# A decoder layer with 32 experts on one core: where in an expert pair the previous pair's combination is issued

## The chip, the cores and the metric

The kernel runs on one core of a Trainium2 chip. The metric is device microseconds of one execution. Engines are called by the profile's names: PE (TensorE matmul), PEld (its weight loads), DVE (VectorE), ACT (ScalarE), POOL (GpSimd) and SP (SyncE, which issues nearly all transfers here).

## The reference, cut to what matters

The layer is an attention mixer on 512 tokens of width 2048, and behind it a mixture of 32 experts. Only the experts matter here:

```
def hierarchical_moe(h, router_g, router_e, w_gate, w_up, w_down):
    ...   # each token: 1 group of 4, 2 of the group's 8 experts, weights `gate`
    def expert_block(args):
        xe, e = args
        u = jax.nn.silu(xe @ w_gate[e]) * (xe @ w_up[e])
        return u @ w_down[e]
    ...
    return jnp.zeros_like(h).at[buf_tok].add(yb * buf_w[:, None].astype(h.dtype))
x = x + g2 * y.reshape(B, S, D)
```

Every expert has three float32 matrices of 4 MB (2048x512, 2048x512, 512x2048). 512 tokens with two experts each make 1024 assignments.

## The kernel before, in words

The instructions of each engine, and the issues on its queue, stand in the order in which the program writes them (`tc.manual_schedule()`); the framework only adds the semaphore waits. Up to about 950 us the kernel does the modulation, the mixer and the router. Then 16 pairs of experts follow (`for n in range(NP)`). In a pair the first 64 columns of a tile belong to expert 2n and the other 64 to expert 2n+1, so that one pair takes up to 64 tokens of each of its experts. Tokens beyond that are done in the block behind `tc.If(reg > 0)`; `reg` counts such blocks, and it is zero for these inputs (no instruction of the block is in the trace).

The steps of pair n, in the order of the program:

- **gates and find.** `gates` (lines 1199 and 1201) computes the token weights of pair n on DVE; `find` (lines 1183 to 1192) builds for pair n+1 the one-hot matrix `oT` and the token indices on DVE, and POOL issues the gather of its rows into `xg` (line 1189).
- **g, in four steps c = 0 to 3.** Each takes two weight tiles of 1 MB (one of each expert) and eight matmuls, which the trace shows as 16 PE instructions of 512 columns. ACT then applies Silu (`gate_fn`).
- **u**, in four steps of the same size. Then `hidden` (DVE, line 1268), `hidden_t` (four PE transposes, line 1274, and an ACT copy to `uT`).
- **y**, in four steps f. In f = 0 and 1 there are also the transposes of the next pair's rows (`turn_x`, line 1211, `ga`), after `normed` (DVE, line 1205). The four sums `py` stand in the four PSUM banks of the tag "mm".
- **gated** (lines 1223 to 1225), once for each quarter q of the columns: DVE computes `yt` out of `py[q]`, ACT copies it to `yH`, DVE computes the rest `yL`.

The **combination** adds `yH + yL` to the tokens' rows: `add_pair` yields four times, once for each q; each time it issues eight PE matmuls (two for each token tile, `cb`) into the four banks of the same tag "mm", and four DVE additions into `acc` (line 1233). It is a generator, `done`, that the next pair advances. Before the change it advances after g step 2, after u step 1, after `hidden`, and after `hidden_t`:

```
                if (k, c) in (("g", 2), ("u", 1)):
                    next(done, None)
...
        u = hidden(sg, pgu[1])
        next(done, None)
        uT = hidden_t(u)
        next(done, None)
        flat(done)
```

The last pair works otherwise: its `w_down` is loaded by column parts, f is a column part, and `last_pair` combines and stores quarter by quarter (line 1247).

**SBUF slots.** All weight tiles and large buffers share 23 slots of 8 KB per partition (pool "big"). While y of a pair runs, ten are taken by the accumulators `acc` (4), the gate row, `rows`, `more`, the two `xg` and the next `xe`, and twelve by weight tiles loaded ahead: `need` loads up to 12 tiles beyond the one in use (`AH = 12`). `yH` takes the 23rd slot, when the last `w_down` tile leaves it. `yL` gets the slot that is given back next. `load_to` (line 256) issues the weight loads on SP, and each issue may wait for its slot and for an earlier transfer on its semaphore lane.

The counts of overflow blocks (`nbk`, `toti`) are computed behind all pairs, and `nc.values_load` (line 1359) reads the number into a register of every engine just before the `If`.

Of the kernel before, what the change touches and what calls it, by code (L numbers as in the profile page):

```python
# [14 lines left out]
I32 = mybir.dt.int32  # L15
AF = mybir.ActivationFunctionType
OP = mybir.AluOpType
AX = mybir.AxisListType
PSUM = bass.MemoryType.PSUM

P = 128
# [4 lines left out]
NE = 32  # L26
# [3 lines left out]
CAP = 64  # L30
# [47 lines left out]
def tile_hybrid_layer(ctx: ExitStack, tc, A, out, dbg=None):  # L78
    nc = tc.nc
    x, xT, w_mod, w_in, w_q_up, rel_bias, w_out = (  # L80
        A[k] for k in ("x", "xT", "w_mod", "w_in", "w_q_up", "rel_bias", "w_out"))
    w_gate, w_up, w_down = A["w_gate"], A["w_up"], A["w_down"]

    sm = ctx.enter_context(tc.tile_pool(name="sm", bufs=1))
# [4 lines left out]
    def slot(shape, dt=F32, name="b"):  # L89
        t = big.tile(shape, dt, name=name, tag="b")  # L90
        return t

    def bank(tag, name, dt=F32):
        t = ps.tile([P, 512], dt, name=name, tag=tag)
        return t

    V, G, T, SC, Q = nc.vector, nc.gpsimd, nc.tensor, nc.scalar, nc.sync

    def act(o, i, f=AF.Copy, **kw):
        return SC.activation(o, i, f, **kw)  # L100

    def mm(o, l, r, start, stop, skip=False):
        return T.matmul(o, l, r, start=start, stop=stop, skip_group_check=skip)  # L103
# [62 lines left out]
    w_g_v = w_gate.rearrange("e (c p j) f -> e c p j f", c=4, j=4)  # L166
    w_u_v = w_up.rearrange("e (c p j) f -> e c p j f", c=4, j=4)
    w_d_v = w_down.rearrange("e (j p) d -> e j p d", p=P)
    w_dc_v = w_down.rearrange("e (j p) d -> e p j d", p=P)

    SH1, SC1, G1, SH2, SC2, G2 = range(6)
    CUTS = {SC2: CUT[0], SH2: CUT[1], G1: CUT[2], G2: CUT[3]}
# [2 lines left out]
    def src(it):  # L175
        k = it[0]
        if k == "m":
            _, v, c, q = it
            if c is None:
                return w_mod_v[:, q, v * D:v * D + D], [P, D]  # L180
            o, n, r = PIECES[c]
            return w_mod_v[:, r * q:r * q + r, v * D + o:v * D + o + n], [P, r, n]
        if k == "A":
            _, c, h = it
            return w_in_v[c][:, h, :, 0:NA], [P, 2, NA]
        if k == "B":
            _, n, c = it
            return w_in_v[c][..., BCOL + 512 * n:BCOL + 512 * (n + 1)], [P, 2, 2, 512]
        if k == "Q":
            return w_q_v[:, :, 512 * it[1]:512 * (it[1] + 1)], [P, 4, 512]  # L190
        if k == "O":
            _, c, q = it
            return w_o_v[:, 4 * q:4 * q + 4, 512 * c:512 * (c + 1)], [P, 4, 512]
        if k == "g":
            return w_g_v[it[1], it[2]], [P, 4, 512]
        if k == "u":
            return w_u_v[it[1], it[2]], [P, 4, 512]
        if it[1] >= NE - 2:
            return w_dc_v[it[1]][..., 512 * it[2]:512 * it[2] + 512], [P, 4, 512]
        return w_d_v[it[1], it[2]], [P, D]  # L200


# [8 lines left out]
    for d, (o, n, r) in enumerate(PIECES):  # L211
# [3 lines left out]
        k = len(mod) // 2 if d else 0  # L215
# [853 lines left out]
    def st(shape, name):  # L1069
        return sm.tile(shape, F32, name=name)  # L1070
# [3 lines left out]
                    op=OP.mult)  # L1074
# [66 lines left out]
    cnt = st([P, 32], "cnt")  # L1141
# [62 lines left out]
    def normed(xs, g, cs=slice(0, D)):  # L1204
        V.tensor_scalar(xs[:, cs], xs[:, cs], g[:, 2:3], None, op0=OP.mult)  # L1205
# [47 lines left out]
    def need(i, k, e, c):  # L1253
        load_to(base + i + 1 + AH)
        return raw.pop((k, e, c))

    def flat(g):
        for _ in g:
            pass

    def gate_fn(pb):
        sg = sm.tile([P, S], F32, name="sg", tag="rb", bufs=2)
        act(sg, pb, AF.Silu)
        return sg

    def hidden(sg, pb):
        u = sm.tile([P, S], F32, name="u", tag="rb", bufs=2)
        V.tensor_tensor(u, sg, pb, op=OP.mult)  # L1268
        return u
# [9 lines left out]
    def down(py, uT, f, ws):  # L1279
        for r in range(2):  # L1280
            hs = slice(64 * r, 64 * r + 64)
            mm(py[hs], uT[:, 128 * f + 64 * r:128 * f + 64 * r + 64], ws[r], f == 0, f == 3, True)

    xe = slot([P, 16, P], name="xe")
    oT, g = find(slotk[:, 0:1], xg[0])
    make_row(rows[:, 2], gt[:, 0])
# [4 lines left out]
    done = iter(())  # L1291
    NP = NE // 2
    for n in range(NP):
        pgu = []
        i = 24 * n
        last = n == NP - 1
        for k in "gu":
            po = bank("at", k)
            pgu.append(po)
            if k == "g":  # L1300
                gate = gates(slotk[:, n:n + 1], g)
                if not last:
                    after = find(slotk[:, n + 1:n + 2], xg[(n + 1) % 2])
            for c in range(4):
                ws = [need(i + r, k, 2 * n + r, c) for r in range(2)]
                i += 2
                for j in range(4):
                    for r in range(2):
                        hs = slice(64 * r, 64 * r + 64)
                        mm(po[hs], xe[:, 4 * c + j, hs], ws[r][:, j], c == 0 and j == 0, c == 3 and j == 3, True)  # L1310
                if (k, c) in (("g", 2), ("u", 1)):
                    next(done, None)
            if k == "g":
                sg = gate_fn(po)
        u = hidden(sg, pgu[1])
        next(done, None)
        uT = hidden_t(u)
        next(done, None)
        flat(done)
        if not last:  # L1320
            normed(xg[(n + 1) % 2], after[1])
            xe = slot([P, 16, P], name="xe")
        py = [bank("mm", f"y{q}") for q in range(4)]
        if last:
            yH, yL = slot([P, D], F32R, name="yH"), slot([P, D], F32R, name="yL")
            done = last_pair(oT, yH, yL)
        for f in range(4):
            ws = [need(i + r, "d", 2 * n + r, f) for r in range(2)]
            i += 2
            if last:  # L1330
                for k in range(4):
                    down(py[f], uT, k, [w[:, k] for w in ws])
                gated(py[f], gate, yH, yL, f)
                for _ in range(4 if f else 0):
                    next(done)
                continue
            for q in range(4):
                down(py[q], uT, f, [w[:, 512 * q:512 * q + 512] for w in ws])
                if q % 2 and f < 2:
                    turn_x(xe, xg[(n + 1) % 2], 2 * f + q // 2)  # L1340
        if last:
            break
        yH, yL = slot([P, D], F32R, name="yH"), slot([P, D], F32R, name="yL")
        for q in range(4):
            gated(py[q], gate, yH, yL, q)
        done = add_pair(oT, yH, yL)
        oT, g = after
    flat(done)


    nbk = st([P, 32], "nbk")
    V.tensor_scalar(nbk, cnt, float(CAP), None, op0=OP.is_gt)
    for b in range(1, 4):
        V.scalar_tensor_tensor(nbk, cnt, float(CAP + 128 * b), nbk, op0=OP.is_gt, op1=OP.add)
    tot = st([P, 1], "tot")
    toti = sm.tile([P, 1], I32, name="toti")
    V.tensor_reduce(tot, nbk, axis=AX.X, op=OP.add)
    V.tensor_copy(toti, tot)
    reg = nc.values_load(toti[0:1, 0:1], min_val=0, max_val=16,
                         skip_runtime_bounds_check_because="1024 assignments fill under 16 such blocks")  # L1360
    with tc.If(reg > 0):
        ov = k2([P, 512], "ov")
        end = ov[:, 0:64].rearrange("p (i e) -> p i e", i=2)
# [4 lines left out]
        for i in range(5):  # L1368
            k, a, b = 1 << i, end[:, i % 2], end[:, (i + 1) % 2]
# [5 lines left out]
        with tc.For_i(0, reg, 1):  # L1375
# [15 lines left out]
                                skip_runtime_bounds_check_because="a count of experts that end before a block")  # L1391
            oT, g = find(oc[:, 4:5], xg[0])
            g = (g, gates(oc[:, 4:5], g))
# [52 lines left out]
def _prepare(inputs):  # L1446
    f = lambda n: np.asarray(inputs[n])
    fold = lambda v: v.reshape(4, 128, 4, -1).transpose(1, 0, 2, 3).reshape(128, -1)
    fold8 = lambda v: v.reshape(8, 128, 2).transpose(1, 0, 2).reshape(128, -1)
    tall = lambda v: v.reshape(-1, 128).T  # L1450
    bm = f("b_mod").reshape(6, 2048)
    vecs = np.concatenate(
        [fold8(bm[1]), fold8(bm[0]), fold(bm[4]), fold(bm[3]), fold8(f("ln1_g")), fold(f("ln2_g")),
         f("c").reshape(128, 16), tall(f("q_norm_g")), tall(f("q_gain")), tall(f("k_gain")), tall(f("gn_a")),
         tall(f("gn_b"))], axis=1)
    cst, ohd, flip = _constants()
    a = {
        "x": f("x").reshape(512, 2048), "xT": f("x").reshape(512, 2048).T, "w_mod": f("w_mod")[0],
        "w_in": f("w_in")[0], "w_q_up": f("w_q_up")[0], "rel_bias": f("rel_bias"),
        "w_out": f("w_out")[0], "w_gate": f("w_gate")[0], "w_up": f("w_up")[0], "w_down": f("w_down")[0],  # L1460
        "router": fold(np.concatenate([f("router_g")[0], f("router_e")[0]], axis=1)), "vecs": vecs, "b_gate": bm[[2, 5]], "cst": cst, "ohd": ohd, "flip": flip,
        "toki": np.tile(np.arange(512, dtype=np.float32) - AWAY, (128, 1)),
    }
    return {k: np.ascontiguousarray(v) for k, v in a.items()}
# [15 lines left out]
```

## Time and profile before

| | |
|---|---|
| Time, median of 3 runs | 1921.93 us (1921.22 to 1929.43) |
| The profiled execution | 1928.09 us, span 1926.2 us |
| Busy, share of the span | PE 92%, DVE 50%, ACT 31%, POOL 20% |
| Granted TensorE clock, mean | 0.978 |
| HBM traffic over the span | 583.60 MB read, 8.40 MB written |
| Weight loads of the experts | 384 transfers of 1024 KB on SP's queue |

The profile's page gives shares over the whole span, and the stages differ: the experts have the transfers at about 420 GB/s in slice after slice, the mixer does not. So the tables by window and the timelines of one pair say more than the shares. A busy PE is not a PE at its peak: each row's duration includes the drain of its pipeline, and the start of the next row is the better measure.

### The profile page before, as it was taken

To read this page: it belongs to the slowest core of one execution; us is meant where nothing else is said; L and a number is where in the kernel's file an instruction comes from. 1 tells how busy PE (TensorE), PEld (TensorE's weight loads), DVE (VectorE), ACT (ScalarE), POOL (GpSimd) and SP (SyncE) were. 2 spreads that over 40 slices of the span, in tenths; PEclk is the share of its full clock that TensorE was granted. 3 is DMA by queue.
4 is the path that set the end of the run, shared out by engine and by line. 5 is a ranking of instruction groups with operands and counts; after the bars stand their busy time and mean duration, and the time that the engine had idled before them with its cause. 6 is when DMAs were issued, how large, how long until landed. Compare 5 with 4: busy or idle time off the path is not lost.

```text
span 1926.2 us, 21350 instructions
## 1 busy us (share of the span) xinstructions
PE 1763.9 (92%) x8098; PEld 986.5 (51%) x8098; DVE 971.9 (50%) x1473; ACT 604.2 (31%) x1138; POOL 394.0 (20%) x307
## 2 busy tenths in 40 slices
PE   4999999999899998898799999999999999999997
PEld 1777777665677676786333333333333333333333
DVE  6888722378855668768322333423333343323325
ACT  3645444554547543443221101111021101211020
POOL 3543311333337326756000000000000000000000
PEclk8999999999999998999799999999999999999999
DMA  9878412323225647769499999999999999999997
GB/s 349 273 260 297 133 66 88 131 88 101 81 104 200 243 175 262 262 250 374 180 420 420 419 419 419 419 420 419 419 419 420 419 419 420 419 420 418 420 414 273
DMA packets 136427, 585.06 MB, mean 304 GB/s; under 512 B 10761, under 2 KB 43697, under 8 KB 78977
## 3 DMA queue, kind: packets, MB, share of 16 engines
q1 hardware_dynamic: 132240, 569.09, 75.3%
q0 software_dynamic: 4080, 14.57, 2.1%
q8 instruction: 65, 1.06, 0.2%
q14 instruction: 42, 0.34, 0.0%
HBM read 583.60 MB, written 8.40 MB: 307 GB/s over the span
## 4 chain that ended last, share of the span: by engine, by line
DMA 44%; PE 6%; DVE 1%; issue 0%; ACT 0%; SPq 0%; DVEq 0%
DMA w_u<-in_w_up 17%; DMA w_g<-in_w_gate 14%; DMA w_d<-in_w_down 14%; PE y L103 2%; PE u L103 2%; PE g L103 1%; PE cb L103 1%; PE ga L1211 0%; DVE x L1233 0%; DMA xg<-x1d,gi 0%; DVE xg L1205 0%; DVE u L1268 0%; PE uT L1274 0%; DVE yt L1223 0%; DVE yL L1225 0%
## 5 line engine op out<-in xcount | busy, mean ns | idle before, releaser
L103 PE MATMUL u<-w_u,xe 128*64 128x512 f32 x1024 | 270.0, 602 | 26.3 <-DMA w_u<-in_w_up 25.2
L103 PE MATMUL g<-w_g,xe 128*64 128x512 f32 x1024 | 242.2, 598 | 21.2 <-DMA w_g<-in_w_gate 21.2
L1233 DVE TENSOR_TENSOR x<-cb,x 128x512 f32<-128x512 f32 x256 | 157.3, 683 | 193.5 <-PE cb L103 193.4
L103 PE MATMUL y<-w_d,uT 128*64 128x512 f32 x1024 | 236.9, 600 | 0.7 <-ACT uT L100 0.7
L282 POOL TENSOR_TENSOR accv<-accv,w_m_None 128x768 f32<-128x768 f32 (+2 forms) x62 | 153.7, 2479 | 217.6 <-ACT w_m_None L100 138.6
L1189 POOL DMA_INDIRECT xg<-x1d,gi x16 | 16.1, 1006 | 875.6 <-DVE t L1192 634.2
L103 PEld LDWEIGHTS u<-w_u,xe 128*64 128x64 f32 x1024 | 79.5, 137 | 206.5 <-issue 135.8
L103 PEld LDWEIGHTS g<-w_g,xe 128*64 128x64 f32 x1024 | 77.1, 137 | 175.5 <-issue 129.3
L1223 DVE SCALAR_TENSOR_TENSOR yt<-y,gs,accv 128x512 f32<-128x512 f32 x64 | 47.8, 747 | 202.4 <-PE y L103 202.4
L280 DVE SCALAR_TENSOR_TENSOR accv<-w_m_None,sil,accv 128x1280 f32<-128x1280 f32 (+2 forms) x62 | 133.9, 2160 | 6.1 <-issue 5.4
L100 ACT ACTIVATE xe<-ga,modc 128x128 f32<-128x128 f32 x256 | 94.6, 465 | 119.8 <-PE y L103 92.6
L103 PEld LDWEIGHTS y<-w_d,uT 128*64 128x64 f32 x1024 | 66.6, 136 | 116.0 <-issue 107.9
L100 ACT ACTIVATE uT<-uT 128x512 f32<-128x512 f32 x16 | 9.6, 598 | 352.3 <-PE uT L1274 352.3
L103 PE MATMUL cb<-yH,oT 128*128 128x512 f32 x256 | 107.8, 421 | 0.9 <-DVE x L1233 0.9
L100 ACT ACTIVATE yH<-yt 128x512 fp32r<-128x512 f32 x64 | 40.4, 631 | 204.6 <-DVE yt L1223 121.5
L103 PE MATMUL cb<-yL,oT 128*128 128x512 f32 x256 | 101.0, 394 | 0.0
L1225 DVE TENSOR_TENSOR yL<-yt,yH 128x512 fp32r<-128x512 f32 x64 | 44.3, 692 | 110.5 <-PE g L103 52.8
L394 DVE TENSOR_TENSOR hl<-w_O,hl 128x1024 fp32r<-128x1024 f32 x32 | 67.8, 2122 | 40.6 <-ACT hl L100 31.7
L1268 DVE TENSOR_TENSOR u<-sg,u 128x512 f32<-128x512 f32 x16 | 11.0, 689 | 130.6 <-PE u L103 130.6
L282 POOL TENSOR_TENSOR acc<-acc,w_m 128x160 f32<-128x160 f32 x105 | 61.3, 584 | 71.5 <-ACT w_m L100 63.8
L103 PEld LDWEIGHTS cb<-yH,oT 128*128 128x128 f32 x256 | 48.2, 188 | 49.6 <-issue 39.5
L1211 PEld LDWEIGHTS ga<-cst,xg 128*128 128x128 f32 x256 | 36.8, 210 | 64.6 <-issue 43.9
(413 smaller groups left out, 3190.0 us busy)
## 6 DMA issues: line engine op xcount, KB each, us to landing
w_g<-in_w_gate SPq DMA_DIRECT2D x128, 1024.0 KB, 19.9
w_u<-in_w_up SPq DMA_DIRECT2D x128, 1024.0 KB, 21.2
w_d<-in_w_down SPq DMA_DIRECT2D x128, 1024.0 KB, 19.9
w_m_None<-in_w_mod SPq DMA_DIRECT2D x64, 1024.0 KB, 5.0
w_m<-in_w_mod SPq DMA_DIRECT2D x32, 1024.0 KB, 9.0
w_B<-in_w_in SPq DMA_DIRECT2D x48, 512.0 KB, 4.7
w_O<-in_w_out SPq DMA_DIRECT2D x16, 1024.0 KB, 5.5
w_A<-in_w_in SPq DMA_DIRECT2D x8, 848.0 KB, 11.3
```

The source lines that it names most:

```text
L100: return SC.activation(o, i, f, **kw)
L103: return T.matmul(o, l, r, start=start, stop=stop, skip_group_check=skip)
L280: V.scalar_tensor_tensor(acc[:, lo], w[:, lo], s, acc[:, lo], op0=OP.mult, op1=OP.add)
L282: G.tensor_tensor(acc[:, hi], acc[:, hi], w[:, hi], op=OP.add)
L394: low_eng[0].tensor_tensor(t[:, 1], s, t[:, 0].bitcast(F32), op=OP.subtract)
L1189: G.indirect_dma_start(xs, None, x1d[:, :], bass.IndirectOffsetOnAxis(ap=gi[:, 0:1], axis=0), bounds_check=S - 1, oob_is_err=False)
L1211: T.transpose(pb[:, 128 * j:128 * j + 128], xs[:, 512 * c:512 * c + 512].rearrange("p (k j) -> p j k", j=4)[:, j], ident)
L1223: V.scalar_tensor_tensor(yt, y, g, rowv[G2][:, cs], op0=OP.mult, op1=OP.mult)
L1225: V.tensor_tensor(yL[:, cs], yt, yH[:, cs].bitcast(F32), op=OP.subtract)
L1233: return lambda: V.tensor_tensor(acc[q][:, t], pb, acc[q][:, t], op=OP.add)
L1268: V.tensor_tensor(u, sg, pb, op=OP.mult)
```

## The change

Four edits:

- The combination of pair n-1 is advanced once after each of the four g steps of pair n, its matmuls and its additions alike; nothing of it is left for u, `hidden` or `hidden_t`.
- The counts of overflow blocks are computed at the head of pair 1.
- The registers are loaded at the head of the last pair, on all engines.
- The last pair's `w_down` comes from a new input `w_last`, which holds the two matrices by column parts; a partition then reads one run of 8 KB for a tile, where it read four runs of 2 KB.

```diff
         if it[1] >= NE - 2:
-            return w_dc_v[it[1]][..., 512 * it[2]:512 * it[2] + 512], [P, 4, 512]
+            return A["w_last"][it[1] - NE + 2, it[2]], [P, 4, 512]
...
+    nbk = st([P, 32], "nbk")
+    def blocks():
+        V.tensor_scalar(nbk, cnt, float(CAP), None, op0=OP.is_gt)
+        for b in range(1, 4):
+            V.scalar_tensor_tensor(nbk, cnt, float(CAP + 128 * b), nbk, op0=OP.is_gt, op1=OP.add)
+        tot = st([P, 1], "tot")
+        toti = sm.tile([P, 1], I32, name="toti")
+        V.tensor_reduce(tot, nbk, axis=AX.X, op=OP.add)
+        V.tensor_copy(toti, tot)
+        return toti
...
     for n in range(NP):
+        if n == 1:
+            toti = blocks()
+        if n == NP - 1:
+            reg = nc.values_load(toti[0:1, 0:1], min_val=0, max_val=16,
+                                 skip_runtime_bounds_check_because="1024 assignments fill under 16 such blocks")
...
-                if (k, c) in (("g", 2), ("u", 1)):
+                if k == "g":
                     next(done, None)
             if k == "g":
                 sg = gate_fn(po)
+        flat(done)
         u = hidden(sg, pgu[1])
-        next(done, None)
         uT = hidden_t(u)
-        next(done, None)
-        flat(done)
...
-    nbk = st([P, 32], "nbk")
-    V.tensor_scalar(nbk, cnt, float(CAP), None, op0=OP.is_gt)
-    ...
-    V.tensor_copy(toti, tot)
-    reg = nc.values_load(toti[0:1, 0:1], min_val=0, max_val=16,
-                         skip_runtime_bounds_check_because="1024 assignments fill under 16 such blocks")
     with tc.If(reg > 0):
...
+        "w_last": f("w_down")[0, -2:].reshape(2, 4, 128, 4, 512).transpose(0, 3, 2, 1, 4),
```

## Rows read from the trace of the kernel before

**Rows 1.** Page, part 4: shares of the span on the chain that ended last.
```profile
DMA 44%; PE 6%; DVE 1%; issue 0%; ACT 0%; SPq 0%; DVEq 0%
```
**Rows 2.** Busy by window, pair 1 and pairs 3 to 13: length, engines, clock, DMA.
```profile
992.09:1049.19 57.10, 55.64 (x246) 22.70 (x244) 21.33 (x39) 9.65 (x22) 1.00 (x1) 1.00 1.01 419
...
1110.65:1788.91 678.26, 634.76 (x2686) 246.20 (x2684) 234.73 (x429) 106.09 (x242) 10.99 (x11) 1.00 1.01 419
```
**Rows 3.** Waits of SP's queue, 1000 to 1840 us: total, times, longest.
```profile
SPq L256 <- DMA w_u<-in_w_up: 255.2, 112, 4.0
```
**Rows 4.** Timeline of DVE around the head of pair 14: start, duration.
```profile
1792.60 0.69 DVE L1225 TENSOR_TENSOR yL<-yt,yH 128x512 fp32r<-128x512 f32 x1 [5.27 <-PE g L103]
...
1797.31 0.75 DVE L1223 SCALAR_TENSOR_TENSOR yt<-y,gs,accv 128x512 f32<-128x512 f32 x1
...
1803.81 2.48 DVE L1233 TENSOR_TENSOR x<-cb,x 128x512 f32<-128x512 f32 x4
```
**Rows 5.** Timeline of PE in the g steps of the same pair.
```profile
1788.91 7.89 PE L103 MATMUL g<-w_g,xe 128*64 128x512 f32 x34
1798.10 3.65 PE L103 MATMUL g<-w_g,xe 128*64 128x512 f32 x14 [1.31 <-DMA w_g<-in_w_gate]
1801.68 0.50 PE L103 MATMUL cb<-yH,oT 128*128 128x512 f32 x1
...
1803.74 3.66 PE L103 MATMUL g<-w_g,xe 128*64 128x512 f32 x16
```
**Rows 6.** Chain that ended last, in pair 0, which has no combination.
```profile
959.02 13.79 PE u L103 x64
...
974.98 1.94 PE y L103 x8
...
985.24 7.04 PE y L103 x32
```
**Rows 7.** Timeline of the last combination: DVE, then PE.
```profile
1914.18 4.87 DVE L1233 TENSOR_TENSOR x<-cb,x 128x512 f32<-128x512 f32 x8
```
**Rows 8.** The same on PE: first and last rows of the group that waits.
```profile
1915.01 0.47 PE L103 MATMUL cb<-yH,oT 128*128 128x512 f32 x1 [0.91 <-DVE x L1233]
...
1917.04 0.39 PE L103 MATMUL cb<-yL,oT 128*128 128x512 f32 x1
```
**Rows 9.** Timeline of all engines, last pair (pair 15).
```profile
1850.04 4.46 PE L103 MATMUL g<-w_g,xe 128*64 128x512 f32 x18
...
1850.91 0.69 DVE L1225 TENSOR_TENSOR yL<-yt,yH 128x512 fp32r<-128x512 f32 x1 [2.44 <-DMA w_g<-in_w_gate]
...
1855.62 0.75 DVE L1223 SCALAR_TENSOR_TENSOR yt<-y,gs,accv 128x512 f32<-128x512 f32 x1
...
1859.13 0.16 DVE L1201 TENSOR_TENSOR gs<-gs 128x1 f32<-128x1 f32 x1
...
1893.67 7.09 PE L103 MATMUL y<-w_d,uT 128*64 128x512 f32 x32
```
**Rows 10.** Issues of the last pair's w_down: ns min/median/max, first and last start.
```profile
L256 SPq DMA_DIRECT2D w_d<-in_w_down x8: 379/2491/8947, 1868.3 to 1892.8; - x8
```
**Rows 11.** Busy by window while these tiles come in.
```profile
1895.00:1900.00 5.00, 5.00 (x26) 1.72 (x24) 1.44 (x2) 0.63 (x1) 0.00 (x0) 1.00 1.03 385
```
**Rows 12.** The end: the count's last step on DVE (timeline).
```profile
1920.06 0.15 DVE L1358 CAST toti<-tot 128x1 int32<-128x1 f32 x1
```
**Rows 13.** Line 1359, the register load, on POOL's queue.
```profile
L1359 POOLq TENSOR_LOAD <-toti x1: 1195/1195/1195, 1920.3 to 1920.3; - x1
```
**Rows 14.** Line 1476, the end of the program, on POOL's queue.
```profile
L1476 POOLq DRAIN x3: 46/103/2518, 1922.8 to 1925.9; - x3
```
**Rows 15.** Line 1247, the stores: from issue to landing.
```profile
DMA to landing us min/median/max: 2.8/3.0/3.3
```
**Rows 16.** A u step of pair 3 on PE.
```profile
1136.70 5.34 PE L103 MATMUL u<-w_u,xe 128*64 128x512 f32 x14 [1.43 <-DMA w_u<-in_w_up]
```
**Rows 17.** Busy by window in the same step; the third figure from the end is the clock.
```profile
1137.00:1140.00 3.00, 3.00 (x10) 0.78 (x8) 0.00 (x0) 0.00 (x0) 0.00 (x0) 0.50 1.02 423
```

More of the change, by code (lines that the diff above doesn't have):

```diff
@@ L168, in tile_hybrid_layer @@
     w_d_v = w_down.rearrange("e (j p) d -> e j p d", p=P)
-    w_dc_v = w_down.rearrange("e (j p) d -> e p j d", p=P)
     SH1, SC1, G1, SH2, SC2, G2 = range(6)
@@ L1348, in tile_hybrid_layer @@
     flat(done)
-    nbk = st([P, 32], "nbk")
-    V.tensor_scalar(nbk, cnt, float(CAP), None, op0=OP.is_gt)
[L1353 to L1357, printed above, removed]
-    V.tensor_copy(toti, tot)
-    reg = nc.values_load(toti[0:1, 0:1], min_val=0, max_val=16,
-                         skip_runtime_bounds_check_because="1024 assignments fill under 16 such blocks")
     with tc.If(reg > 0):
```

## Prediction

> **What bounds the kernel now.** I read the page's chain of waits first: 44% of the span on it are weight transfers, 6% PE, 1% DVE [rows 1]. That share is the expert stage. The table by window gives the stage's pace: about 419 GB/s and a DMA share of 1.01 whatever PE does [rows 2]. The waits of SP's queue say how this looks at the issuing end: an issue waits for an earlier transfer, 112 times for w_u alone [rows 3]. The reader should see one more thing in rows 2: pair 1 took 57.10 us while a lead of loaded tiles was used up; pairs 3 to 13 took 678.26/11 = 61.66 us each. So PE's own pace is at most 57.1 us, and transfers set about 61.3: from the first g matmul of pair 1 at 992.09 [rows 2] to that of pair 15 at 1850.04 [rows 9] are 857.95 us for 14 pairs, 61.28 us each. PE has some 4 us to spare in a pair. Only at the very end, from the last u tiles on, is PE and then DVE the bound.
>
> So the question is whether PE's own pace stays under 61.3 us when the combination moves. I work it out from the timelines of one pair, with G the start of its g.
>
> **The combination behind g, in pairs 1 to 14.** Nothing of it is removed: 32 matmuls and 16 additions a pair go elsewhere. What changes is what they wait for.
>
> 1. DVE at the head of a pair. yL of the first quarter starts at 1792.60 and has waited 5.27 us, until g's first step was through [rows 4, 5]: its slot is the one that this step gives back, since ten buffers, twelve tiles ahead and yH fill the 23. The change leaves that count as it is, as the old yH and yL are gone by then either way. From there DVE runs without a hole: the last yt ends at 1797.31+0.75 = 1798.06, G+9.15, and gates and find end where the first addition starts, 1803.81, G+14.90 [rows 4]. These stand ahead of the additions in DVE's queue, before and after.
>
> 2. First quarter, now behind g step 0. A step to the next start takes 3.58 us and a quarter's eight matmuls 2.06 [rows 5]. Its four token tiles need the four "mm" banks, which yt empties one by one: the fourth can start at G+9.2, so g step 1 starts near G+9.75 and not G+3.6, and ends at G+13.3.
>
> 3. Second quarter, behind g step 1. It needs the same banks, emptied by the first quarter's additions, and these start at G+14.90 only. The last pair's combination shows this pattern: additions from 1914.18 [rows 7], PE goes on at 1915.01 after a wait and starts its last matmul at 1917.04, +0.33 to the next instruction [rows 8]: 3.19 us. So g step 2 starts at 14.90+3.19 = G+18.09. Before, the first quarter came behind step 2 at 1801.68, G+12.77 [rows 5], when the banks had long been emptied, and the others in u and behind it.
>
> 4. The rest streams: 3.58+2.06+3.58+2.06 = 11.28, u starts at G+29.37. Its 64 instructions take 13.79, and from their end at 972.81 to y's start 974.98 are 2.17 [rows 6]: in pair 0 nothing covers hidden and the transposes, and after the change nothing does in any pair. y starts at G+45.33. y with the transposes takes 992.09-974.98 = 17.11 [rows 2, 6]. Sum: 62.44 us a pair.
>
> That is above 61.28: PE, not the transfers, would set the pace, by 1.16 us a pair, 16.2 us over 14 pairs. The counts of overflow blocks put six operations (1.16 us, from the end of the additions at 1919.05 to the end of the cast at 1920.21 [rows 7, 12]) ahead of find in pair 1: +1.2. Together +17.4. Transfers don't suffer: a tile then lies unused for up to 13 us, so that the queue is issued later, but a tile that arrives 20 us before its use, as those of u would, has room. An error of 0.5 us in the 62.44 (a matmul's drain, a drifting order of the last bank) is 7 us in the sum.
>
> The Trainium skill (Perfetto Trace Analysis, Matmuls) wants independent matmul groups to rotate through different PSUM banks so that emptying one overlaps the next group's matmuls. A quarter takes all four banks of its tag, and the trace agrees with the rule at the only place where quarters follow closely: 0.91 us of waiting [rows 8]. The sum above doesn't rest on the rule.
>
> **The last pair.** It has no find, and its yL found a slot at once (1850.91, 0.87 after G) [rows 9]. The register load costs each queue about 1.2 us [rows 13]; on PE it stands before g step 0 and is hidden, since the banks hold the first quarter until the last yt at 1856.37, G+6.33 [rows 9]. On SP it stands among issues that wait for transfers, on POOL and ACT before nothing urgent; if SP's cover went, 1.2 us. On DVE it stands ahead of gates: these ended at 1859.29, G+9.25 [rows 9]; with it G+10.5. Then as in 3 and 4: 10.5+3.19+11.28+13.79+2.17 = y at G+40.9. Before it was 1893.67, G+43.63: three of the four quarters lay between the last g and y. From y on nothing changes, so 2.7 us are won. If transfers still set the pace: a tile takes 2.5 us at 419 GB/s [rows 2], step 0 has its two near G, the last of u's comes 14 tiles or 35 us later, some 3.2 us of matmuls and 2.2 for hidden follow, and y starts near G+41 too: the gain is the same.
>
> **w_down by column parts.** Issues of these tiles took 0.4 to 8.9 us on SP [rows 10] and the rate was 385 GB/s [rows 11] against 419 [rows 2]: 8.39 MB in 21.8 and not 20.0 us. I cost it at nothing: y in rows 9 runs without a wait for a tile. With y 2.7 us earlier the old layout would have been late by at most that; between 0 and 2 us, and I take 0.
>
> **The end.** The last addition ends at 1919.05 [rows 7], the span at 1926.2: 7.15 us. On it lie the count's 1.16, the register load (1.20 from 1920.3 [rows 13]), and POOL's drain of 2.52 us from 1922.8 [rows 14]. With the register known, POOL drains early. What is late next is the last store: 0.4 us of issue and 3.0 to landing [rows 15] end near 1922.4, with the closing semaphores of SP behind it, which filled some 3 us before. The gain is between 0.5 and 2.5; I take 1.5.
>
> **Sum.** +17.4 -2.7 -1.5 = +13.2 us on the profiled execution's 1928.09: 1941.3. The median of the runs is 1921.93, 6.2 lower. If transfers made that difference, a kernel paced by PE doesn't get it back; if an earlier stage did, it would come to 1935. I take 1938, between them; own range 1930 to 1951.
>
> **The rivals.**
>
> *The transfers stay the bound* (27%). If yL got a slot at once, as in pair 15, DVE would be 2.8 us earlier throughout (0.87 against 3.69 after G), the first quarter's hold-up would be 2.8 us less and 62.44 become 59.6, under 61.28. For it: rows 9 show the case. Against it: 5.27 us in rows 4 and the same count of slots in every other pair. The edits at the end then stand alone: -4.2, 1918 by the median. At 61.3 to 61.9 a pair, between, it comes out within 0.5% as well.
>
> *The clock falls at the new holes* (14%). PE would work 1.8 us of the 6.2 between g step 0 and step 1, and 1.8 of the next 4.8 behind step 1. In pair 3, after waits for tiles, the granted clock was 0.50 of full speed, its lower level of 1.2 GHz, for 3 us, and 14 instructions took 5.34 us where 3.65 is usual [rows 16, 17, 5]: 1.7 us. One such fall in each of 14 pairs is +24: 1962. Against it: pairs 3 to 13, each with waits for tiles, have a mean clock of 1.00 [rows 2]. The Trainium skill (TensorE: Matmul & The Clock Gate, psum-queue depth-cycling) tells of a kernel whose PE idled briefly between groups while cycling through PSUM and whose clock swung between its levels. The one fall in the rows followed waits for transfers, so no row here shows its case.
>
> *A larger gain* (5%): the early layout and the two ends together save over 9.6 us. PE's chain after the last w_u tile and the last store leave no room for it that I see.
>
> The rival on the other side of my forecast is the first; it decides at a PE pace of 61.3 us a pair.
>
> **How the numbers follow.** PE at 62.4 us a pair 54%, transfers as before 27%, clock falls 14%, a larger gain 5%. 0.5%, 9.6 us, is what a measurement of this kernel tells from no change. Faster is the 5%; same is the transfers' 27% and the part of the forecast's range below 1931.5, 3%; slower is the rest, 65%. The range for eight in ten takes in the transfers' case and one fall a pair: 1916 to 1963.
>
> **What would show it.** Timelines of a middle pair: g steps 1 and 2 starting near G+9.8 and G+18.1, ended by waits for DVE (yt, then the additions); G to G 62.4 us; about 2.2 us between u and y; DMA below 419 GB/s; SP's waits turning from transfers to PE. At the end: PE's y 41 us after G of pair 15, the span's end 5 to 6 us behind the last addition. It is wrong if pairs still take 61.3 us, if yL no longer waits for g step 0, or if additions run ahead of find.

## The result and the profile after

The kernel with the change takes 1946.91 us (median, 1942.65 to 1953.67) against 1921.58 for the kernel before on the same chip: ratio 1.0119 [1.0092, 1.0147]. It is slower. The profiled execution took 1942.65 us with a span of 1940.9 (before: 1928.09 and 1926.2).

The page's chain of waits is no help this time. It breaks off behind the last additions, and the 44% of [rows 1] are gone from it, which doesn't mean that the waits are gone:

```profile
DVE 0%; issue 0%
```

So I go by the other views. First busy time by window, as in [rows 2] (length, then PE, PEld, DVE, ACT, POOL; clock; DMA share; GB/s): pair 1, and pairs 3 to 13.

```profile
987.13:1051.12 63.99, 58.22 (x246) 21.60 (x244) 22.40 (x45) 9.62 (x22) 1.00 (x1) 0.95 1.01 415
...
1114.30:1805.12 690.82, 635.09 (x2686) 238.06 (x2684) 235.43 (x429) 105.85 (x242) 10.96 (x11) 0.96 1.00 409
```

Pair 1 no longer runs ahead (63.99 us where [rows 2] have 57.10), pairs 3 to 13 take 690.82/11 = 62.80, and the rate is 409 GB/s, not 419. Second, the waits of SP's queue from 1000 to 1840 us, which answer to [rows 3]:

```profile
SPq L255 <- PE g L103: 344.1, 55, 12.5
SPq L255 <- PE y L103: 178.2, 53, 4.7
SPq L255 <- PE u L103: 137.2, 53, 3.0
```

An issue now waits for PE to give back a tile, where it waited for earlier transfers: PE sets the pace. Third, PE in pair 14, as in [rows 5], through to the next pair's g:

```profile
1805.12 3.60 PE L103 MATMUL g<-w_g,xe 128*64 128x512 f32 x16
...
1809.56 0.51 PE L103 MATMUL cb<-yL,oT 128*128 128x512 f32 x1 [0.40 <-DVE yL L1224]
...
1812.36 0.47 PE L103 MATMUL cb<-yH,oT 128*128 128x512 f32 x1 [1.34 <-DVE yt L1222]
...
1814.41 0.76 PE L103 MATMUL cb<-yH,oT 128*128 128x512 f32 x1 [1.35 <-DVE yt L1222]
1814.97 0.63 PE L103 MATMUL cb<-yL,oT 128*128 128x512 f32 x1
1815.53 4.60 PE L103 MATMUL g<-w_g,xe 128*64 128x512 f32 x16
1820.85 0.47 PE L103 MATMUL cb<-yH,oT 128*128 128x512 f32 x1 [0.71 <-DVE x L1232]
...
1823.21 3.65 PE L103 MATMUL g<-w_g,xe 128*64 128x512 f32 x16
...
1834.51 13.95 PE L103 MATMUL u<-w_u,xe 128*64 128x512 f32 x64
...
1849.35 0.66 PE L1273 MATMUL uT<-cst,u 128*128 128x128 f32 x4 [0.89 <-DVE u L1267]
1850.75 1.94 PE L103 MATMUL y<-w_d,uT 128*64 128x512 f32 x8 [0.75 <-ACT uT L100]
...
1867.85 3.60 PE L103 MATMUL g<-w_g,xe 128*64 128x512 f32 x16
```

Between g's first step and its second PE waits for yt after yt; behind the second it waits for DVE's first addition; behind u it waits for hidden and for the transposes' copies. On DVE the same pair reads as in [rows 4], 16 us later on the clock and the same after G:

```profile
1808.81 0.69 DVE L1224 TENSOR_TENSOR yL<-yt,yH 128x512 fp32r<-128x512 f32 x1 [5.27 <-PE g L103]
...
1813.52 0.75 DVE L1222 SCALAR_TENSOR_TENSOR yt<-y,gs,accv 128x512 f32<-128x512 f32 x1
...
1820.01 4.87 DVE L1232 TENSOR_TENSOR x<-cb,x 128x512 f32<-128x512 f32 x8
```

The last pair, as in [rows 9], got shorter. PE first, then DVE's register load and its last additions (to hold against [rows 7]):

```profile
1867.85 3.60 PE L103 MATMUL g<-w_g,xe 128*64 128x512 f32 x16
...
1908.07 7.09 PE L103 MATMUL y<-w_d,uT 128*64 128x512 f32 x32 [0.69 <-ACT uT L100]
```
```profile
L1309 DVEq TENSOR_LOAD <-toti x1: 545/545/545, 1874.9 to 1874.9; - x1
```
```profile
1928.58 4.87 DVE L1232 TENSOR_TENSOR x<-cb,x 128x512 f32<-128x512 f32 x8
```

The last w_down tiles come at the stage's full rate, against 385 GB/s in [rows 11], and their issues on SP are short, against [rows 10]:

```profile
1895.00:1900.00 5.00, 5.00 (x26) 1.67 (x24) 0.00 (x0) 0.00 (x0) 0.00 (x0) 1.00 1.01 419
```
```profile
L255 SPq DMA_DIRECT2D w_d<-in_w_last x8: 327/355/1036, 1884.3 to 1896.0; - x8
```

At the very end POOL's long drain is over 100 us early (in [rows 14] it began at 1922.8), but the stores land later than in [rows 15]:

```profile
L1482 POOLq DRAIN  x3: 46/103/8662, 1821.9 to 1940.6; - x3
```
```profile
DMA to landing us min/median/max: 2.8/3.9/4.8
```

Where the span went, with G1 and G15 the starts of g in pairs 1 and 15:

| stretch | before | after | difference | predicted |
|---|---|---|---|---|
| start to G1 | 992.09 | 987.13 | -5.0 | 0 |
| G1 to G15, 14 pairs | 857.95 | 880.72 | +22.8 | +17.4 |
| G15 to the last addition's end | 69.01 | 65.60 | -3.4 | -2.7 |
| from there to the span's end | 7.15 | 7.45 | +0.3 | -1.5 |

From G1 on it is +19.7 us. The first row is work that the change doesn't touch (in the profiled executions of all the kernels here it took 987.1 to 998.0 us), so in these two executions 5 us of it are hidden. The medians lie 25.3 apart; the 10.8 us between that and the profiled executions' 14.6 fall in executions that left no trace.

### The profile page after: what moved, and what is told of

It reads as the page before. It is cut to its first block, busy times and chain, and to the rows that moved or that the text cites. A ratio compares the mean times of both kernels' runs of the same rounds, so it can differ in the third digit from the quotient of the medians.

```text
span 1940.9 us, 21263 instructions
## 1 busy us (share of the span) xinstructions
PE 1760.1 (91%) x8098; PEld 972.5 (50%) x8098; DVE 972.8 (50%) x1473; ACT 602.8 (31%) x1138; POOL 393.8 (20%) x307
## 5 line engine op out<-in xcount | busy, mean ns | idle before, releaser
L103 PE MATMUL g<-w_g,xe 128*64 128x512 f32 x1024 | 256.8, 649 | 0.0
L103 PE MATMUL u<-w_u,xe 128*64 128x512 f32 x1024 | 223.2, 594 | 0.0
L103 PE MATMUL cb<-yH,oT 128*128 128x512 f32 x256 | 118.1, 461 | 45.7 <-DVE yt L1222 40.7
L103 PEld LDWEIGHTS u<-w_u,xe 128*64 128x64 f32 x1024 | 72.1, 137 | 143.2 <-issue 138.5
L103 PE MATMUL cb<-yL,oT 128*128 128x512 f32 x256 | 106.5, 416 | 5.8 <-DVE yL L1224 5.8
L100 ACT ACTIVATE sg<-g 128x512 f32<-128x512 f32 x16 | 9.6, 598 | 275.1 <-PE g L103 275.1
L281 POOL TENSOR_TENSOR acc<-acc,w_m 128x160 f32<-128x160 f32 x105 | 61.1, 582 | 70.6 <-ACT w_m L100 62.9
## 6 DMA issues: line engine op xcount, KB each, us to landing
w_d<-in_w_down SPq DMA_DIRECT2D x120, 1024.0 KB, 10.9
```

The lines of the kernel that those rows point to most:

```text
L281: G.tensor_tensor(acc[:, hi], acc[:, hi], w[:, hi], op=OP.add)
```

## The experiments

**The move alone, and all but the move.** My theory: the move makes PE the bound, and the other edits are worth a few us. The rival: the early counts, the register load or the new layout upset the stage. `all but the move` is the changed kernel with the combination's place as before:

```diff
-                if k == "g":
+                if (k, c) in (("g", 2), ("u", 1)):
                     next(done, None)
...
-        flat(done)
         u = hidden(sg, pgu[1])
+        next(done, None)
         uT = hidden_t(u)
+        next(done, None)
+        flat(done)
```

`move only` is the kernel before with this edit reversed.

> All edits of the change but the move: a pair's combination is advanced where it was before (after g step 2, u step 1, hidden, hidden_t); early counts, early registers and the new layout of the last w_down stay. Theory (the move makes PE the bound, through the waits for the banks behind g steps 0 and 1): pairs 1 to 14 from g to g take 61.3 us on average, the last addition comes 69 us after the last pair's g, and the time is that of the kernel before within 4 us, 1918 to 1924. Rival (the cost is in the other edits: layout, register loads in the middle of the work): it stays near the changed kernel's, 1940 or more.

> Only the move: the combination is advanced after each g step; counts and registers come at the end and w_down is laid out as before. Theory: pairs take 62.7 to 63.2 us from g to g, g step 2 starts 18.1 us or more after g, and the time is that of the changed kernel within 5 us, 1940 to 1952. Rival (the cost is in the other edits): 1918 to 1924.

All but the move: 1926.7 us against 1927.29, ratio 0.9990 [0.9967, 1.0013]; its 14 pairs took 857.51 us. The move only: 1944.92, ratio 1.0094 [1.0059, 1.0130]; 880.46 us for 14 pairs. So the loss is the move's. The other edits give nothing that can be told from zero. (The first figure lies above what I had stated, and so does the kernel before on that chip; the ratio is as expected.)

**One tile less ahead.** Is yL's wait for g's first step what holds PE back? With eleven tiles ahead yL has a slot at once.

```diff
-    AH = 12
+    AH = 11
```

> The changed kernel with 11 tiles loaded ahead where there are 12: a slot is then free for yL at once. Theory (DVE's start at the head of a pair is set by yL's slot, and the later waits by DVE): yL starts about 0.9 us after g and not 3.7, g step 1 about 7 and not 10.4, g step 2 about 15.3 and not 18.1; PE's own pace falls to about 60 us, under the transfers' 61.3, and the time to 1914 to 1924. Rival 1 (the falls of the clock are the cost): they stay, since the holes stay, and the time stays over 1938. Rival 2 (fewer tiles ahead starve PE): over 1950.

1925.02 us, ratio 0.9999 [0.9981, 1.0018]: the loss is gone. (The time is a little above the one that I had stated; the kernel before took 1927.29 us on that chip.) DVE and PE in pair 14:

```profile
1789.65 0.69 DVE L1224 TENSOR_TENSOR yL<-yt,yH 128x512 fp32r<-128x512 f32 x1 [2.44 <-ACT yH L100]
```
```profile
1788.78 3.60 PE L103 MATMUL g<-w_g,xe 128*64 128x512 f32 x16
...
1795.89 3.65 PE L103 MATMUL g<-w_g,xe 128*64 128x512 f32 x16
1801.67 0.47 PE L103 MATMUL cb<-yH,oT 128*128 128x512 f32 x1 [2.13 <-DVE x L1232]
...
1804.53 4.71 PE L103 MATMUL g<-w_g,xe 128*64 128x512 f32 x16
...
1850.22 3.60 PE L103 MATMUL g<-w_g,xe 128*64 128x512 f32 x16
```

yL starts at G+0.87 and not G+3.69, step 1 at G+7.11 and not G+10.41, step 2 at G+15.75 and not G+18.09. But the pair takes 61.44 us, more than the 59.6 that my first rival had for this case. 1.6 us of that are a fall of the clock, which shows here in step 2 (4.71 us, not 3.65) and in the quarter ahead of it (2.86 us from 1801.67 to 1804.53, where the changed kernel takes 2.36). Pair 7 shows the case without a fall: 59.89 us at a mean clock of 1.00 (below, busy by window for pairs 7 and 14).

```profile
1360.69:1420.58 59.89, 54.84 (x246) 21.02 (x244) 21.40 (x39) 9.73 (x22) 1.00 (x1) 1.00 1.01 417
1788.78:1850.22 61.44, 56.40 (x247) 21.50 (x245) 21.40 (x39) 10.37 (x23) 1.00 (x1) 0.97 1.01 419
```

**Later steps.** If the banks and the additions are what PE waits for, quarters at steps where both are done should cost nothing, though hidden and the transposes stay uncovered.

```diff
-                if k == "g":
+                if (k, c) in (("g", 2), ("g", 3), ("u", 0), ("u", 1)):
```

> The changed kernel with the four quarters of the combination behind g steps 2 and 3 and u steps 0 and 1. Theory: behind g step 2 (10.7 us after g) all banks are empty, and the second quarter behind g step 3 (about 16.4) finds them emptied by the additions that start at 14.9, so no wait over 0.5 us is left in g; what is left is the 2.2 us of hidden and the transposes. PE's own pace is about 59 us, the pairs take 61.3, the clock stays at 1.00, and the time is 1914 to 1922. Rival (what costs is the uncovered hidden and transposes, which stay): pairs above 62 us and a time over 1930.

> The kernel with the quarters behind g steps 2 and 3 and u steps 0 and 1, once more in more rounds, to see if it is faster than the kernel before. Theory (pairs at the transfers' pace, the last addition some 3 us earlier): 0.2% faster than before, 1917 to 1926 us, with an interval below 1. Rival (nothing is left of the gain): a ratio of 1.000 within 0.0015.

1924.96 us, ratio 0.9981 [0.9963, 0.9999]; run again 1925.21, 0.9989 [0.9971, 1.0007]. PE waits for tiles of w_g once more (the first line is the total of its waits over the 14 pairs in us, their number and the longest), and the 1.6 us behind u are still there, and are harmless:

```profile
PE g L103 <- DMA w_g<-in_w_gate: 44.1, 37, 1.9
```
```profile
1792.63 3.65 PE L103 MATMUL g<-w_g,xe 128*64 128x512 f32 x16 [1.34 <-DMA w_g<-in_w_gate]
...
1828.31 0.66 PE L1273 MATMUL uT<-cst,u 128*128 128x128 f32 x4 [0.85 <-DVE u L1267]
1829.71 1.94 PE L103 MATMUL y<-w_d,uT 128*64 128x512 f32 x8 [0.75 <-ACT uT L100]
```

So with later quarters nothing is lost, although hidden and the transposes stay uncovered: PE has time to spare for them. In the changed kernel it has none, and there the same 1.6 us stand in the pair's 62.73. Without them the pair would come to 61.1 us by my estimate (62.73-1.64), the transfers' own pace. No run covered that place while it left the quarters where the change puts them, so the loss is the sum of PE's waits, and that the two at the banks alone are to blame isn't shown. Whether this version is faster than the kernel before stays unclear: the second interval takes in 1, and that ratio fits the rival's 1.000 within 0.0015 as well.

**Additions ahead of find.** The second wait, behind step 1, is for additions that stand behind gates and find in DVE's queue. This kernel emits gates and find after the first quarter.

```diff
-            if k == "g":
-                gate = gates(slotk[:, n:n + 1], g)
-                if not last:
-                    after = find(slotk[:, n + 1:n + 2], xg[(n + 1) % 2])
...
                     next(done, None)
+                if (k, c) == ("g", 0):
+                    gate = gates(slotk[:, n:n + 1], g)
+                    if not last:
+                        after = find(slotk[:, n + 1:n + 2], xg[(n + 1) % 2])
```

> The changed kernel with gates and find behind the first quarter's combination, so that this quarter's additions stand ahead of them in DVE's queue. Theory (the second wait is for DVE's queue order): the additions start about 10.6 us after g and not 14.9, the second quarter finds its banks empty, and g step 2 starts about 16.1 us after g if the clock holds and 17.3 to 18 if it falls in step 1 as it does in the changed kernel (then the fall, hidden before behind the wait, shows). Pairs take 60.7 to 62.2 us, or the transfers' 61.3; time 1917 to 1934. Rival (banks and yt alone are the cost, DVE's order is not): pairs stay at 62.7 and the time over 1938.

1942.87 us, ratio 1.0074 [1.0048, 1.0101]: my expected time was missed, and the rival's came, but not the rival's pairs of 62.7 us. The 14 pairs took 872.71 us, 62.34 each, which is 8 us less than in the changed kernel; in this execution g of pair 1 began at 997.98, 10.9 later than there, and that hides it in the execution's time. DVE and PE in pair 14 show half of the theory:

```profile
1818.78 2.48 DVE L1232 TENSOR_TENSOR x<-cb,x 128x512 f32<-128x512 f32 x4
```
```profile
1808.33 3.60 PE L103 MATMUL g<-w_g,xe 128*64 128x512 f32 x16
...
1818.75 5.32 PE L103 MATMUL g<-w_g,xe 128*64 128x512 f32 x16
```

The additions start at G+10.45, not G+14.89, and PE's wait behind step 1 is gone. But step 1 takes 5.32 us instead of 3.65. The clock there, busy by window as above:

```profile
1819.00:1822.00 3.00, 3.00 (x8) 0.74 (x8) 3.00 (x7) 0.00 (x0) 0.00 (x0) 0.50 1.01 421
```

So step 2 starts at G+17.73, only 0.36 us earlier than in the changed kernel (over the 14 pairs it starts at G+17.01 to G+18.63). The changed kernel has this fall too, in step 1 of each of its 14 pairs: the step takes 4.6 to 6.1 us there (4.60 in pair 14, above). The question was then what it costs.

**The holes filled.** Two matmuls whose results nobody uses go ahead of each of the third and fourth token tiles of the first quarter, where PE waits for yt.

```diff
-            for f in [combine(oT, yH, yL, q, t, "mm") for t in range(4)]:
+            fs = []
+            dm = bank("at", "dm") if q == 0 else None
+            for t in range(4):
+                if q == 0 and t > 1:
+                    for _ in range(2):
+                        mm(dm[0:64], ident[:, 0:64], rows[:, 0], True, True, True)
+                fs.append(combine(oT, yH, yL, q, t, "mm"))
+            for f in fs:
```

> The changed kernel with two idle matmuls (results unused) ahead of the third and of the fourth token tile of the first quarter, where PE waits 1.3 us each for yt. Theory (a fall of the clock in g step 1 hides behind the additions, which start 14.9 us after g whatever PE does): the clock stays at 1.00 in step 1, which takes 3.6 us, step 2 still starts about 18.1 us after g, pairs take 62.4 to 62.7, and the time is that of the changed kernel within 5 us, 1936 to 1950. Rival (the falls of the clock are what the move costs): pairs go back to 61.3 and the time below 1930.

1950.36 us, ratio 1.0134 [1.0088, 1.0179], as slow as the change. The clock stands at 1.00 from pair 2 on, and it buys next to nothing:

```profile
1110.00:1840.00 730.00, 689.79 (x2928) 255.08 (x2930) 255.01 (x466) 110.45 (x251) 11.96 (x12) 1.00 1.00 410
```
```profile
1818.17 3.65 PE L103 MATMUL g<-w_g,xe 128*64 128x512 f32 x16
1823.02 0.47 PE L103 MATMUL cb<-yH,oT 128*128 128x512 f32 x1 [1.20 <-DVE x L1232]
...
1825.39 3.65 PE L103 MATMUL g<-w_g,xe 128*64 128x512 f32 x16
```

Step 1 is at full speed again, then PE waits 1.20 us for the additions instead of 0.71. Step 2 starts at G+18.09, as without the filling; 14 pairs took 880.89 us (880.72). That is the sum of two small differences: pairs 2 to 14 took 1.4 us less in all, and pair 1, where the clock did fall in step 2, 1.6 us more. Of the time, 2.6 us are the last pair's (68.19 us from G15 to the last addition, 65.60 in the changed kernel), which has the extra matmuls too: 3.7 us of work, where PE had waited 1.27 us for yt. In the changed kernel, then, the falls are nearly all hidden behind the wait for the additions.

**Both.** If the wait and the fall hide each other, neither cure alone can take the loss away, and the two together must. This is `additions ahead of find` with the extra matmuls, except in the last pair.

> Both at once: gates and find behind the first quarter's combination, and the two idle matmuls each ahead of its third and fourth token tiles (none in the last pair). Theory (three things make up the loss: banks held until yt, the additions behind find, and, once that second wait is gone, the fall of the clock in step 1): the clock stays at 1.00, step 1 takes 3.6 us and starts 10.9 us after g, step 2 starts about 16.5, PE's own pace is 61.1 us, pairs take the transfers' 61.3 to 61.5, and the time is 1917 to 1930. Rival (something else slowed the kernel with find later, say its later gather): pairs stay above 62 us and the time above 1934.

1922.17 us against 1927.16, ratio 0.9969 [0.9952, 0.9986]: 0.3% faster than the kernel before. Step 2 is at step 1 plus 5.64, nothing waits behind step 1, and the 14 pairs take 857.81 us, at the transfers' rate of 419 GB/s. But it is still PE that sets their pace, just at that of the transfers: pairs 1 to 13 took 61.17 to 61.25 us each, and in the 14 pairs PE waited for a weight tile once, in pair 14. The second block below is that wait (total, times, longest), to hold against the 44.1 us with later quarters.

```profile
1110.00:1840.00 730.00, 701.79 (x3002) 264.10 (x2998) 256.86 (x468) 111.50 (x254) 11.96 (x12) 1.00 1.01 419
```
```profile
PE g L103 <- DMA w_g<-in_w_gate: 1.2, 1, 1.2
```
```profile
1800.33 3.65 PE L103 MATMUL g<-w_g,xe 128*64 128x512 f32 x16
1805.97 3.65 PE L103 MATMUL g<-w_g,xe 128*64 128x512 f32 x16
```

Its trace shows 1.4 us of that gain in the last pair (67.57 us from G15 to the last addition, before 69.01) and gives 0.35 back at the end; the rest of the 5 us isn't in the two profiled executions and stays open.

**The end.** Two kernels, both with the later steps. The first computes the counts and loads the registers at the end, as before; the second keeps them early and brings back the four runs of 2 KB. Each has one execution, the profiled one (1928.47 and 1926.62 us), so only their traces are used.

```diff
-        if n == 1:
-            toti = blocks()
-        if n == NP - 1:
-            reg = nc.values_load(toti[0:1, 0:1], ...)
...
+    toti = blocks()
+    reg = nc.values_load(toti[0:1, 0:1], ...)
```
```diff
-            return A["w_last"][it[1] - NE + 2, it[2]], [P, 4, 512]
+            return w_down.rearrange("e (j p) d -> e p j d", p=P)[it[1]][..., 512 * it[2]:512 * it[2] + 512], [P, 4, 512]
```

> The kernel with the quarters behind g steps 2 and 3 and u steps 0 and 1, with counts and register load back at the end. Theory A (the early register shortens the end by what lay on it, but late landing of the last stores gives it back): the stores land 3.0 to 3.6 us after issue as in the two kernels that load late, and the end lies 7.2 us behind the last addition. Theory B (the late landing comes with the new layout of w_down): stores still land 3.7 to 4.8 us after issue, and the end lies 7.2 to 8.5 us behind the last addition.

> The kernel with the quarters behind g steps 2 and 3 and u steps 0 and 1, with early register and the old layout of the last w_down. Theory A (late landing comes with the early register): stores land 3.7 to 4.8 us after issue, the end lies 7.3 us behind the last addition. Theory B (it comes with the new layout): they land 3.0 to 3.6 us after issue and the end lies 5.5 to 6 us behind the last addition. In both, the issues of w_down on SP take 2.5 us again and the last addition comes at most 2 us later after the last pair's g than with the new layout.

Over all eight stores the landing times mix two things: the first two stores, issued 14 to 15 us ahead of the last, take 3.5 to 5.0 us, early register or late. So I read the last four alone. With the late register they land like this, and from the last addition to the span's end are 7.14 us:

```profile
DMA to landing us min/median/max: 2.8/3.1/3.4
```

With the early register and the old layout:

```profile
DMA to landing us min/median/max: 2.8/4.7/4.8
```

and 7.4 us. The last three stores land after 4.6 to 4.9 us in all nine kernels here that load the register early, and after 3.0 to 3.4 in the three that load it late (the kernel before, the move only, late register). The late landing goes with the early register and not with the layout. Why a store lands later when the register was loaded long before it is not shown and stays open. With the old layout the stretch from G15 to the last addition took 70.0 us, with the new one 69.44 and 69.60 in two executions of the same kernel. That is 0.4 to 0.6 us for the new layout, within what single profiles differ by.

## Why the prediction was right, point by point

**PE at 62.4 us a pair: right.** The pair measured takes 62.73. DVE's head is as worked out (yL at G+3.69, last yt done at G+9.15, additions at G+14.89), and so are step 2 at G+18.09 and u at G+29.39; y is at G+45.63, 0.3 late. Three experiments carry the mechanism: with an earlier yL, with later quarters, and with earlier additions at full clock the loss is gone.

**Step 1 at G+9.75: 0.66 us too early** (G+10.41). The lines at 1814.41 and 1814.97 are slow, 0.76 and 0.63 us where 0.47 and 0.40 are usual: the fall of the clock begins here, at the end of the quarter, with 0.50 granted from 1814.40 to 1815.50. It cost nothing in this pair, since step 2 waits for the additions.

**14 pairs, +17.4: too small by 5.4.** Ten pairs took 62.71 to 62.74 us, 0.3 over 62.44; over all 14 that is 4.1. The 0.3 lies between u and y: 16.24 us (1834.51 to 1850.75), where the sum had 13.79+2.17 = 15.96. Part of it is a misreading: the chain's row in [rows 6] begins at 959.02, but PE's timeline has the first of these u instructions at 958.85, so that pair 0 shows 16.13. Pair 1 took 63.99, 1.3 over these, which is the counts with their 1.2. Pairs 2, 7 and 12 took 63.13 to 63.18, 1.3 in all, since a fall of the clock outgrew its cover there. Step 1 of pair 2:

```profile
1061.54 6.12 PE L103 MATMUL g<-w_g,xe 128*64 128x512 f32 x16
```

**The clock-fall rival: its events happened, its price did not.** Each of pairs 1 to 14 had one fall, from the end of the quarter in which PE waited for yt into the step after it. In that step of pair 2 the granted clock was 0.50 of full speed, the 1.2 GHz level, as in [rows 17]:

```profile
1062.00:1065.00 3.00, 3.00 (x8) 0.71 (x6) 2.90 (x8) 0.00 (x0) 0.00 (x0) 0.50 1.01 421
```

I had priced it at 1.7 us a pair on top of the sum. The filled holes show that it comes to next to nothing as long as the additions end last. The kernel with additions ahead of find shows that it costs 1.7 us once they don't: step 1 took 4.61 to 6.23 us there, 5.31 on average, and not 3.65. The Trainium skill (TensorE: Matmul & The Clock Gate, psum-queue depth-cycling) describes this: PE idling briefly between groups as it goes through PSUM, the clock swinging between its levels, and throughput lost to it. The trace agrees with the swing (0.50 in one step, 1.00 over the filled stage) but not with a loss in the changed kernel (880.72 us for 14 pairs, 880.89 with the clock at 1.00 in all but one of them). With additions ahead of find there is a loss: 872.71 us, and 857.81 at full clock.

**The transfers-stay-the-bound rival** fell, as yL did wait 5.27 us. Its own figure for the case without that wait, 59.6 us a pair, left out the clock: with one tile less the pair took 61.44 us with a fall, and 59.89 in the one pair without. In that kernel too PE stays just over the transfers' 61.3, so "same" is all that a slot at once could give.

**The last pair, -2.7: measured -3.4.** The register load on DVE (0.55 us, not the 1.2 of [rows 13]) ran beside the last yL, and the additions started at 1877.06, G+9.21, where I had G+10.5. The second quarter then had no wait at all: step 2 started at G+12.74, when step 1 and the quarter were through, and not 3.19 behind the additions' start. y started at G+40.2 (G+40.9).

**The end, -1.5: the step that failed.** It came to +0.3. I took the last store's landing from [rows 15] as it was, 3.0 us. Drain, counts and load did go from the end, but the last store, issued at 1933.47, landed after 4.7 us: 4.72 behind the last addition, where it had been 3.35 before. That is 1.4 of the 1.8 us. The closing work behind the landing took 2.7 us, where my 1.5 left 2.3 for it. A small term, but of the wrong sign; why the store lands late stays open.

In the profiled execution the misses nearly cancel, by luck: +5.4 for the pairs, +1.8 for the end, -0.7 for the last pair, -5.0 for the start, so 1942.65 against the sum of 1941.3. I had gone 3.3 us below that sum because the median of before lay 6.2 below its profiled execution; the median of after lies 4.3 above its own. These two are 7.6 of the 8.9 us between 1938 and 1946.91; the rest is the sum's own miss.

## What to carry to other kernels

Before moving PE work to an earlier place, ask of each operand and each bank when the other engine, with its queue in the order in which it stands, will have made or emptied it: here the quarters had fitted from G+12.8 on, and begun at G+3.6 they cost 1.6 us a pair. Where two waits lie behind each other, a cure for one can show no gain, or uncover the next; test them together before dropping either. Of an epilogue's steps, the one that is late next has to be read under the new conditions, not from the old row.

## What the runs showed of the hardware that I had not expected

The same step of 16 g matmuls took 3.65 us at a clock of 1.00, and 4.6 to 6.2 us after a quarter in which PE waited between pairs of matmuls; two short unused matmuls in each of two such waits kept the clock at 1.00 (in all 14 pairs of one kernel and in 13 of the other). The register load took 0.46 to 0.55 us in mid-kernel, where the engines came to it one after another, and 1.1 to 1.2 us at the end, where all five did so at once. The last three stores landed after 3.0 to 3.4 us where the register was loaded late, and after 4.6 to 4.9 where it was loaded early.
